# Retention's transpositions in one visit of three banks, HGRN2's heads side by side, and sample phases set apart: a decoder layer in fp32 on one core

## The chip, the core and the metric

The kernel runs on one core of a Trainium2 chip. The metric is the device time of one execution in microseconds (us). Five engines work side by side, each in its own instruction order: TensorE (PE, with its weight loads as PEld), VectorE (DVE), ScalarE (ACT), GpSimd (POOL) and SyncE (SP), which here only issues DMA transfers. They meet through semaphores. TensorE writes to PSUM, which has eight banks of 2 KB per partition.

## The reference

One layer of a hybrid decoder is computed in fp32 for two groups of requests: a prompt (16 learned meta tokens and 256 prompt tokens) and 8 sample tokens that continue states given as input.

```python
x = layer_norm(ALPHA * x + 0.5 * swiglu(x, f1_g, f1_u, f1_d), ln1_g, ln1_b)
m, s_ret, s_hg = token_mixer(x, pos, s_ret, s_hg, prompt, w_in, lb, hg_norm_g, w_out)
x = layer_norm(ALPHA * x + m, ln2_g, ln2_b)
x = layer_norm(ALPHA * x + 0.5 * swiglu(x, f2_g, f2_u, f2_d), ln3_g, ln3_b)

# token_mixer
q_r, k_r, v_r, g_r, q_h, f_h, i_h, g_h, a_r, a_h = jnp.split(x @ w_in, N_PROJ, axis=-1)
...
# retention (8 heads of 256) and HGRN2 (16 heads of 128), each over chunks:
S_new = jnp.exp(lg * C)[:, None, None] * S + jnp.einsum('bhjd,bhjv->bhdv', k_dec, v)
S_new = jnp.exp(b_last[:, :, 0, :, None]) * S + jnp.einsum('bhjd,bhjv->bhdv', k_dec, v)
...
o_r = head_layer_norm(...) * silu(g_r);  o_h = head_rms_norm(...) * silu(g_h)
y = sigmoid(a_r) * o_r + sigmoid(a_h) * o_h
return y @ w_out, s_ret, s_hg
```

D_MODEL is 2048, the FFN's inner width 5504. Outputs are y of prompt and samples, and the states of both mixers for prompt and samples. A sample's state is read from memory (retention 256x256 for each head and sample, HGRN2 128x128), updated by its token, read with its query, and written back.

## The kernel before

**Layout.** x lies transposed, features on the partitions and all tokens as 280 columns (16 meta, 256 prompt, 8 samples). Each fp32 value is split in two parts, so each 128x128 block of weights costs three matmuls: high weights by high x (L203), high by low (L204), low by high (L205). Weights are streamed in units of eight blocks: SP issues a load of 512 KB to `raw` (L176), ScalarE casts the high part `whi` (L177), VectorE subtracts for the low part `wlo` (L178). There are three buffers of each.

**Stages.** FFN 1 runs to about 740 us, then the input projection `w_in` with the mixers to about 1935 us, then `w_out` and FFN 2.

**The mixers run between the projection's matmuls.** There are eight units u, each of one retention head and two HGRN2 heads. For each unit `project` (L576) computes six groups of projections (f, q_h, i_h, q_r, k_r, v_r), then the gates of unit u−1. A group has two outputs, and 16 steps over the contracted dimension. After each step (six matmuls on 264 or 280 columns) it calls `pump` (L564): a pump counts down every running generator and lets those that are due emit their next piece. So `yield 11` in a mixer means: go on after 11 pumps. A steady unit has 160 pumps, 96 of its own groups and 64 of the gates of the unit before. Unit 0 has its groups of four outputs and no gates before it. What a mixer puts on TensorE between two projection matmuls is called a visit here.

`mix_hg` starts after the i group, `mix_ret` after the v_r group. `mix_hg` transposes v (`pt`), works through the levels of its chunked product (`pl`), transposes K for each head (`ptk`, L830), forms the prompt state (`pst`, L845), reads the samples' states (`pq`, L858), forms the output (`po`, L869 to L871) and its norm's sums (`pv`, L216). It does so for head 0, then for head 1: `ptk` of head 1 comes 31 pumps after that of head 0. In each round, after `ptk`, the head's eight sample states `smp` are updated: eight operations on ScalarE (L836) and eight on VectorE (L837), then the store. Head 1's states are loaded after `pq` of head 0 (L780 for the row of v, L781 for the state), into the same buffer. `mix_ret` transposes v and k for one half of the 256 features at a time, two banks each, in two visits four pumps apart (L894, L900); then scores (`psc`), prompt state (`psr`), outputs (`por`). Then come the samples in two halves of four: `load` (L915, L918), `update` (L923 on ScalarE, L926 on VectorE; two buffers `smr`, c = 0 and 1), `read` (`pqr`, L936). Then `pos`, the mean (`pm`) and the variance (`pvr`). All of that ends before the unit's gates have ended.

**What sets the order.** TensorE's order is the program's own. On ScalarE, VectorE, GpSimd and SP a scheduler places the instructions, and each engine then keeps to that order. PSUM is two pools of four banks: `acc` for the projections, `mx` in rotation for all banks of the mixers (`mx_bank`, L132), so that a fifth bank asked for is the first one again. `smr` has three buffers, which it shares with retention's decayed keys `ktr`; `smp` has one buffer for the state, which it shares with another tile of HGRN2.

## Time and profile before

| what | before |
|---|---|
| device time, median of 3 runs | 2792.39 us (2792.33 to 2794.63) |
| the profiled execution, own time | 2793.12 us |
| its span, first to last instruction | 2791.3 us |
| mean granted clock of TensorE | 0.998 |
| ACT, busy share | 49%, weight casts (L177) 909.5 us |
| DVE, busy share | 61%, weight subtractions (L178) 1063.6 us |
| HBM traffic | 191 GB/s over the span |

In the 40 slices of the span, VectorE is busy four to five tenths in the FFNs and six to seven in the mixers' stage, ScalarE four and five to six. Weights come at a steady 174 GB/s in the FFNs, and traffic rises to between 187 and 256 in the mixers' stage, where the samples' states go in and out besides.

In a row of the timeline stand start, duration, engine, line, operation, output<-input and shapes, and in brackets how long the engine had been idle before and what ended that. In a row of waits stand the waiting engine, tile and line, then what it waited for; then the total, the number of waits and the longest. Line numbers of the profile are those of the kernel before; in the changed kernel the lines of this stretch lie one or more further down.

### The profile page before, as it was taken

The page shows a single profiled execution, that of the slowest core. Times are in us where ns is not written, and L with a number is a line of the kernel's source. Part 1 is how long each engine was busy: PE and PEld are TensorE (multiplying, and loading weights), DVE is VectorE, ACT ScalarE, POOL GpSimd, SP SyncE. Part 2 cuts the span into 40 slices and gives each one's busy share as a digit, 9 for nine tenths or more (in the row PEclk, how much of TensorE's full clock was granted, in tenths as well). Part 3 has the DMA queues.
Part 4 walks back from the last instruction along what each step waited for, and adds up shares of the span by engine and source line. Part 5 has one row for each costly group of instructions (what it writes and reads, how often), then busy time and mean ns, then how long its engine had stood idle before and what let it go on. Part 6 is the DMA issues. An engine that isn't in the chain of part 4 may idle for free.

```text
span 2791.3 us, 55438 instructions
## 1 busy us (share of the span) xinstructions
PE 2761.4 (99%) x22992; PEld 2718.2 (97%) x22992; DVE 1711.4 (61%) x2957; ACT 1360.7 (49%) x2157; POOL 5.5 (0%) x47
## 2 busy tenths in 40 slices
PE   9999999999999899999999999999999999999999
PEld 9999999999999899899999998999999999999998
DVE  6444444555478677676767676766884444446554
ACT  5444434434355565656565656564554444444333
POOL 0000000000000000000000000000000000000000
PEclk9999999999999999999999999999999999999999
DMA  7555555555556576657675757575555565555664
GB/s 234 174 174 174 174 174 173 169 174 174 175 172 225 191 243 199 226 195 237 187 238 185 241 185 241 175 256 176 180 179 184 182 183 184 184 182 182 183 184 141
DMA packets 156460, 536.33 MB, mean 192 GB/s; under 512 B 18032, under 2 KB 27824, under 8 KB 156208
## 3 DMA queue, kind: packets, MB, share of 16 engines
q1 hardware_dynamic: 156064, 532.65, 60.3%
q8 instruction: 180, 2.95, 0.4%
q14 instruction: 72, 0.59, 0.1%
q10 hardware_dynamic: 144, 0.14, 0.0%
HBM read 502.12 MB, written 30.61 MB: 191 GB/s over the span
## 4 chain that ended last, share of the span: by engine, by line
PE 91%; DMA 3%; DVE 3%; ACT 2%; issue 1%; SPq 0%; ACTq 0%; DVEq 0%
PE up L204 12%; PE up L203 12%; PE up L205 12%; PE dn L204 6%; PE dn L203 6%; PE dn L205 6%; DMA smp<-in_sg 2%; PE pj_k_r L203 1%; DMA smr<-in_sr 1%; PE pj_v_r L203 1%; DVE wlo L178 1%; PE pj_f L204 1%; PE pj_f L205 1%; PE pj_k_r L204 1%; PE pj_k_r L205 1%; PE pj_v_r L204 1%
## 5 line engine op out<-in xcount | busy, mean ns | idle before, releaser
L178 DVE TENSOR_TENSOR wlo<-raw,whi 128x1024 fp32r<-128x1024 f32 (+1 forms) x871 | 1063.6, 1221 | 894.6 <-ACT whi L177 886.7
L177 ACT CAST whi<-raw 128x1024 fp32r<-128x1024 f32 (+1 forms) x871 | 909.5, 1044 | 1038.0 <-PE up L204 472.3
L204 PE MATMUL up<-x,whi 128*128 128x280 f32 (+1 forms) x2688 | 773.1, 288 | 0.0
L203 PE MATMUL up<-x,whi 128*128 128x280 f32 (+1 forms) x2688 | 766.3, 285 | 0.6 <-ACT whi L177 0.6
L205 PE MATMUL up<-x,wlo 128*128 128x280 f32 (+1 forms) x2688 | 764.0, 284 | 0.4 <-DVE wlo L178 0.4
L203 PEld LDWEIGHTS up<-x,whi 128*128 128x128 f32 x2688 | 504.9, 188 | 0.9 <-ACT whi L177 0.9
L205 PEld LDWEIGHTS up<-x,wlo 128*128 128x128 f32 x2688 | 505.0, 188 | 0.8 <-DVE wlo L178 0.7
L204 PEld LDWEIGHTS up<-x,whi 128*128 128x128 f32 x2688 | 504.5, 188 | 0.0
L204 PE MATMUL dn<-h,whi 128*128 128x280 f32 (+1 forms) x1376 | 395.6, 287 | 0.0
L203 PE MATMUL dn<-h,whi 128*128 128x280 f32 (+1 forms) x1376 | 392.6, 285 | 0.0
L205 PE MATMUL dn<-h,wlo 128*128 128x280 f32 (+1 forms) x1376 | 390.8, 284 | 0.0
L203 PEld LDWEIGHTS dn<-h,whi 128*128 128x128 f32 x1376 | 258.5, 188 | 0.1
L205 PEld LDWEIGHTS dn<-h,wlo 128*128 128x128 f32 x1376 | 258.5, 188 | 0.0
L204 PEld LDWEIGHTS dn<-h,whi 128*128 128x128 f32 x1376 | 258.3, 188 | 0.1
L203 PE MATMUL pj_g_h<-x,whi 128*128 128x264 f32 x256 | 76.6, 299 | 0.0
L203 PE MATMUL pj_g_r<-x,whi 128*128 128x264 f32 x256 | 76.2, 298 | 0.0
L203 PE MATMUL pj_k_r<-x,whi 128*128 128x280 f32 x256 | 75.1, 293 | 0.0
L205 PE MATMUL pj_i_h<-x,wlo 128*128 128x280 f32 x256 | 74.4, 291 | 0.5 <-DVE wlo L178 0.5
L204 PE MATMUL pj_i_h<-x,whi 128*128 128x280 f32 x256 | 74.5, 291 | 0.0
L204 PE MATMUL pj_k_r<-x,whi 128*128 128x280 f32 x256 | 74.5, 291 | 0.0
L204 PE MATMUL pj_v_r<-x,whi 128*128 128x280 f32 x256 | 74.5, 291 | 0.0
L203 PE MATMUL pj_v_r<-x,whi 128*128 128x280 f32 x256 | 74.5, 291 | 0.0
(377 smaller groups left out, 5207.0 us busy)
## 6 DMA issues: line engine op xcount, KB each, us to landing
raw<-in_w_up SPq DMA_DIRECT2D x341, 512.0 KB
raw<-in_w_in SPq DMA_DIRECT2D x320, 512.0 KB
raw<-in_w_dn SPq DMA_DIRECT2D x172, 512.0 KB
smr<-in_sr SPq DMA_DIRECT2D x32, 512.0 KB
out_srs<-smr SPq DMA_DIRECT2D x32, 512.0 KB
raw<-in_w_out SPq DMA_DIRECT2D x32, 512.0 KB
smp<-in_sg SPq DMA_DIRECT2D x16, 512.0 KB
vbr<-vrd SPq DMA_DIRECT2D x16, 512.0 KB
```

Of the source, the lines that this page charges most:

```text
L177: nc.scalar.copy(hi[:, j0:j1, :], raw[:, j0:j1, :])
L178: nc.vector.tensor_tensor(out=lo[:, j0:j1, :], in0=raw[:, j0:j1, :], in1=hi[:, j0:j1, :].bitcast(F32), op=ALU.subtract)
L203: nc.tensor.matmul(o, wh, h, start=k == 0, stop=False)
L204: nc.tensor.matmul(o, wh, l, start=False, stop=False)
L205: nc.tensor.matmul(o, wl, h, start=False, stop=k == nk - 1)
```

## The change

Four things are done together. The arithmetic stays the same, and TensorE keeps its number of instructions.

1. Retention's 12 transpositions of a unit go into one visit: v's blocks into bank `pv`, k's into `pk`, both tails into a third, `pt`. Each bank is emptied 256 or 512 columns at a time, in place of 128 or 256.
2. In `mix_hg` the two heads go side by side: `ptk` of both, then `pst` of both, `po` of both, `pv` of both. Only the samples stay one after the other. `update` becomes a function: head 0's stands ahead of `ptk`, head 1's 12 pumps after its load. Some tiles get a copy for the second head.
3. Retention's sample phases are set apart from the outputs by APART pumps: 34 in units 2 to 6, 32 in unit 0, 52 in unit 1, none in unit 7. They then run in the next unit's f, q_h and i_h groups.
4. HGRN2's start in unit 1 waits 24 pumps in place of 36.

```diff
+APART = {0: 32, 1: 52, 7: 0, 2: 34}
...
-            start(mix_hg(c0 // 2, st["f"], st["k"], st["q"], v), {0: 3, 2: 36}.get(c0, 3))
+            start(mix_hg(c0 // 2, st["f"], st["k"], st["q"], v), {0: 3, 2: 24}.get(c0, 3))
...
+        def update(h, vb, sm):
+            for b in range(NS):
+                nc.scalar.activation(sm[:, b, :], sm[:, b, :], AF.Copy, scale=fs[:, h, b : b + 1])
+                nc.vector.scalar_tensor_tensor(
+                    out=sm[:, b, :], in0=vb[:, b, :], scalar=ks[:, h, b : b + 1], in1=sm[:, b, :],
+                    op0=ALU.mult, op1=ALU.add)
+            nc.sync.dma_start(O["sgs"][2 * u + h], sm)
...
         Tt = dT[P]
+        update(0, *samples)
         yield W_LEVEL
         on = tmp("on_h", (P, 2, TL), bufs=2)
         on_h[u] = on
+        kt = [tmp("kth", (P, 2, P)) for h in range(2)]
         for h in range(2):
-            kt = tmp("kth", (P, 2, P))
             pt = mx_bank("ptk")
             for b, (t0, n) in enumerate(((NMETA, P), (NMETA + P, P), (0, NMETA))):
                 nc.tensor.transpose(pt[:n, b * P : (b + 1) * P], K[:, h, t0 : t0 + n], ident)
-            nc.scalar.copy(kt, pt[:, : 2 * P].rearrange("p (b f) -> p b f", b=2))
-            stack(lambda r: km3[r, :], pt[:NMETA, 2 * P : 3 * P], 64)
-
-            vb, sm = samples
-            for b in range(NS):
-                nc.scalar.activation(sm[:, b, :], sm[:, b, :], AF.Copy, scale=fs[:, h, b : b + 1])
-                nc.vector.scalar_tensor_tensor(
-                    out=sm[:, b, :], in0=vb[:, b, :], scalar=ks[:, h, b : b + 1], in1=sm[:, b, :],
-                    op0=ALU.mult, op1=ALU.add)
-            nc.sync.dma_start(O["sgs"][2 * u + h], sm)
-            yield 11
-
-            S = tmp("Sh", (P, 3, P))
+            stack(lambda r: km3[r, h, :], pt[:NMETA, 2 * P : 3 * P], 64)
+            nc.scalar.copy(kt[h], pt[:, : 2 * P].rearrange("p (b f) -> p b f", b=2))
+        yield 11
+
+        S = [tmp("Sh", (P, 3, P)), tmp("Sh1", (P, 3, P), tag="K")]
+        for h in range(2):
             pst = mx_bank("pst")
-            nc.tensor.matmul(pst[:, 0:P], km3, vm3[:, h, :], start=True, stop=True)
-            nc.tensor.matmul(pst[:, P : 2 * P], kt[:, 0, :], vt[:, h, 0, :], start=True, stop=True)
-            nc.tensor.matmul(pst[:, 2 * P : 3 * P], kt[:, 1, :], vt[:, h, 1, :], start=True, stop=True)
-            nc.scalar.copy(S[:, 0, :], pst[:, :P])
+            nc.tensor.matmul(pst[:, 0:P], km3[:, h, :], vm3[:, h, :], start=True, stop=True)
+            nc.tensor.matmul(pst[:, P : 2 * P], kt[h][:, 0, :], vt[:, h, 0, :], start=True, stop=True)
+            nc.tensor.matmul(pst[:, 2 * P : 3 * P], kt[h][:, 1, :], vt[:, h, 1, :], start=True, stop=True)
+            nc.scalar.copy(S[h][:, 0, :], pst[:, :P])
             for b in range(2):
                 nc.vector.scalar_tensor_tensor(
-                    out=S[:, b + 1, :], in0=S[:, b, :], scalar=Tt[:, h, b : b + 1],
+                    out=S[h][:, b + 1, :], in0=S[h][:, b, :], scalar=Tt[:, h, b : b + 1],
                     in1=pst[:, (b + 1) * P : (b + 2) * P], op0=ALU.mult, op1=ALU.add)
-            nc.sync.dma_start(O["sgp"][2 * u + h], S[:, 2, :])
-            yield 10
+            nc.sync.dma_start(O["sgp"][2 * u + h], S[h][:, 2, :])
+        yield 4
+        os = tmp("osh", (P, 2, P))
+        for h in range(2):
             pq = mx_bank("pq")
             for b in range(NS):
                 j = 32 * (b % 4)
                 nc.tensor.matmul(
-                    pq[j : j + 32, :P], qdh[:, h, 32 * b : 32 * b + 32], sm[:, b, :],
+                    pq[j : j + 32, :P], qdh[:, h, 32 * b : 32 * b + 32], samples[1][:, b, :],
                     start=b < 4, stop=b >= 4, tile_position=(0, j))
-            os = tmp("osh", (P, P))
-            nc.scalar.copy(os, pq[:, :P])
+            nc.scalar.copy(os[:, h, :], pq[:, :P])
             if h == 0:
                 samples = load(1)
-            yield 3
+                yield 12
+                update(1, *samples)
+                yield 11
+        yield 4
+        hilo = []
+        for h in range(2):
             po = mx_bank("po")
             for b in range(2):
                 o = po[:, b * P : (b + 1) * P]
                 nc.tensor.matmul(o, vt[:, h, b, :], acc[:, (2 * h + b) * P : (2 * h + b + 1) * P], start=True, stop=False)
-                nc.tensor.matmul(o, S[:, b, :], Q[:, h, b * P : (b + 1) * P], start=False, stop=True)
-            nc.tensor.matmul(po[:, SEQ:TL], os, sel, start=True, stop=True)
+                nc.tensor.matmul(o, S[h][:, b, :], Q[:, h, b * P : (b + 1) * P], start=False, stop=True)
+            nc.tensor.matmul(po[:, SEQ:TL], os[:, h, :], sel, start=True, stop=True)
             sq = tmp("sqh", (P, TL))
             nc.scalar.activation(sq, po[:, :TL], AF.Square)
-            hilo = tmp("hhi", (P, TL), dt=F32R), tmp("hlo", (P, TL), dt=F32R)
-            split(*hilo, sq)
+            hilo.append((tmp("hhi", (P, TL), dt=F32R), tmp("hlo", (P, TL), dt=F32R)))
+            split(*hilo[h], sq)
             nc.scalar.copy(on[:, h, :], po[:, :TL])
-            yield 7
-            pv = mx_bank("pv")
-            sums(pv[:, :TL], hilo)
-            r = rsqrt(lambda name: tmp(name, (P, TL)), pv[:, :TL], 1.0 / P, eps_h)
+        yield 7
+        pv = [mx_bank("pv") for h in range(2)]
+        for h in range(2):
+            sums(pv[h][:, :TL], hilo[h])
+        for h in range(2):
+            r = rsqrt(lambda name: tmp(name, (P, TL)), pv[h][:, :TL], 1.0 / P, eps_h)
             mul(on[:, h, :], on[:, h, :], r)
         done_h.add(u)
...
-        for c in range(2):
-            pt = mx_bank("pt")
+        pv, pk, pt = mx_bank("pt"), mx_bank("pt"), mx_bank("pt")
+        for x, p, p2 in ((v, pv, pt[:, : 2 * P]), (k, pk, pt[:, 2 * P :])):
             for b, (t0, n) in enumerate(BLOCKS):
-                nc.tensor.transpose(pt[:n, b * P : (b + 1) * P], v[:, c, t0 : t0 + n], ident)
-            split(vh[:, :, c, :], vl[:, :, c, :], pt[:, : 2 * P].rearrange("p (b f) -> p b f", b=2))
-            nc.scalar.copy(vtl[: BLOCKS[2][1], c, :], pt[: BLOCKS[2][1], 2 * P : 3 * P])
-            stack(lambda r: vs3[r, c, :], vtl[:NB2, c, :], 32)
-            pt = mx_bank("pt")
-            for b, (t0, n) in enumerate(BLOCKS):
-                nc.tensor.transpose(pt[:n, b * P : (b + 1) * P], k[:, c, t0 : t0 + n], ident)
-            for b in range(2):
-                kb, d = pt[:, b * P : (b + 1) * P], dec[:, b, u : u + 1]
-                nc.vector.tensor_scalar(out=kh[:, b, c, :], in0=kb, scalar1=d, scalar2=None, op0=ALU.mult)
-                nc.vector.scalar_tensor_tensor(
-                    out=kl[:, b, c, :], in0=kb, scalar=d, in1=kh[:, b, c, :].bitcast(F32), op0=ALU.mult, op1=ALU.subtract)
-            ktl = tmp("ktl", (P, P))
-            nc.scalar.activation(ktl[:NB2, :], pt[:NB2, 2 * P : 3 * P], AF.Copy, scale=dec[:NB2, 2, u : u + 1])
-            stack(lambda r: ks3[r, c, :], ktl[:NB2, :], 64)
-            yield 4
+                for c in range(2):
+                    at = (2 * b + c if b < 2 else c) * P
+                    nc.tensor.transpose((p if b < 2 else p2)[:n, at : at + P], x[:, c, t0 : t0 + n], ident)
+        flat = [x.rearrange("p b c f -> p (b c f)") for x in (vh, vl)]
+        split(*flat, pv)
+        nc.scalar.copy(vtl[: BLOCKS[2][1]], pt[: BLOCKS[2][1], : 2 * P].rearrange("p (c f) -> p c f", c=2))
+        stack(lambda r: vs3[r], vtl[:NB2], 32)
+        for b in range(2):
+            kb, d = pk[:, 2 * b * P : 2 * (b + 1) * P], dec[:, b, u : u + 1]
+            hi, lo = (x[:, b].rearrange("p c f -> p (c f)") for x in (kh, kl))
+            nc.vector.tensor_scalar(out=hi, in0=kb, scalar1=d, scalar2=None, op0=ALU.mult)
+            nc.vector.scalar_tensor_tensor(out=lo, in0=kb, scalar=d, in1=hi.bitcast(F32), op0=ALU.mult, op1=ALU.subtract)
+        ktl = tmp("ktl", (P, 2, P))
+        nc.scalar.activation(
+            ktl[:NB2], pt[:NB2, 2 * P :].rearrange("p (c f) -> p c f", c=2), AF.Copy, scale=dec[:NB2, 2, u : u + 1])
+        stack(lambda r: ks3[r], ktl[:NB2], 64)
+        yield 8
...
-        first = load(0)
+        apart = APART.get(u, APART[2])
+        if not apart:
+            first = load(0)
         psc = mx_bank("psc")
...
+        if apart:
+            yield apart
+            first = load(0)
+            yield 10
         update(0, *first)
         yield 6
         os = tmp("osr", (P, 256))
```

The first place is on ScalarE in unit 3, around the visit with `ptk` and retention's transpositions; `whi` are weight casts, `v` retention's values, `kth` and `km3` copies of `ptk`, `vtr`, `vtl` and `ktl` copies of retention's banks. Before:

```order
L624 COPY v_16392<-pj_v_r8_16249 128x280
L177 CAST whi170_16538<-raw170_16537 128x1024
L625 COPY v_16392<-pj_v_r9_16250 128x280
L831 COPY kth_16422<-ptk_16423 128x256
L559 CAST km3_8603<-ptk_16423 16x128
L560 CAST km3_8603<-ptk_16423 16x128
L210 CAST vtr_16448<-pt_16455 128x2x128
L177 CAST whi171_16596<-raw171_16595 128x1024
```

After:

```order
L178 CAST whi170_16469<-raw170_16468 128x1024
L626 COPY v_16347<-pj_v_r9_16188 128x280
L560 CAST km3_8603<-ptk_16379 16x128
L561 CAST km3_8603<-ptk_16379 16x128
L560 CAST km3_8603<-ptk_16387 16x128
L561 CAST km3_8603<-ptk_16387 16x128
L843 COPY kth_16377<-ptk_16379 128x256
L211 CAST vtr_16395<-pt_16402 128x512
L843 COPY kth_16378<-ptk_16387 128x256
L911 COPY vtl_16397<-pt_16404 24x256
L919 ACTIVATE ktl_16427<-pt_16404,dec_87 16x256
L178 CAST whi171_16521<-raw171_16520 128x1024
```

Both heads' `km3` and `kth` now come together, the casts for `km3` ahead of the copy `kth`, and `vtr` stands between the two copies.

The same place on TensorE, after the change (before, `ptk` of head 0 was followed by two banks of three transpositions, and two more came four pumps later):

```order
L841 MATMUL ptk_16379<-ident_77,K_15812 128x128 x2
L841 MATMUL ptk_16379<-ident_77,K_15812 16x128
L841 MATMUL ptk_16387<-ident_77,K_15812 128x128 x2
L841 MATMUL ptk_16387<-ident_77,K_15812 16x128
L908 MATMUL pt_16402<-ident_77,v_16347 128x128 x4
L908 MATMUL pt_16404<-ident_77,v_16347 24x128 x2
L908 MATMUL pt_16403<-ident_77,k_r_16178 128x128 x4
L908 MATMUL pt_16404<-ident_77,k_r_16178 24x128 x2
```

Five banks are written in one visit; the third of retention's, `pt_16404`, is the fifth.

The second place is the second halves of the samples in unit 3. First ScalarE, around the update of retention's second half, c = 1 (`smr`). Before:

```order
L836 ACTIVATE smp_16769<-smp_16769,fks_15877 128x128 x2
L177 CAST whi180_17077<-raw180_17076 128x1024
L836 ACTIVATE smp_16769<-smp_16769,fks_15877 128x128 x3
L923 ACTIVATE smr_16829<-smr_16829 128x1024
L177 CAST whi181_17117<-raw181_17116 128x1024
L848 COPY Sh_17028<-pst_17029 128x128
```

After, for the same samples:

```order
L178 CAST whi188_17275<-raw188_17274 128x1024
L1005 COPY osr_17188<-pqr_17189 128x256
L178 CAST whi189_17317<-raw189_17316 128x1024
L936 ACTIVATE smr_17202<-smr_17202 128x1024
L597 ACTIVATE f_17265<-pj_f10_17114 128x280
L178 CAST whi190_17347<-raw190_17346 128x1024
L597 ACTIVATE f_17265<-pj_f11_17115 128x280
```

The update of `smr` stood behind five of head 1's `smp`; it now stands among the next unit's weight casts and f, and no `smp` is near.

Then SP, where head 1's states (`smp`) and retention's second half (`smr`) are loaded. Before:

```order
L915 DMA vbr_16826<-vrd_16562 128x1024
L780 DMA smp_16769<-vh1d_15912 128x1024
L176 DMA raw179_17016<-in_w_in 128x1024
L781 DMA smp_16769<-in_sg 128x1024
L918 DMA smr_16829<-in_sr 128x1024
L176 DMA raw180_17076<-in_w_in 128x1024
```

After:

```order
L177 DMA raw177_16815<-in_w_in 128x1024
L782 DMA smp_16630<-vh1d_15850 128x1024
L783 DMA smp_16630<-in_sg 128x1024
L177 DMA raw178_16845<-in_w_in 128x1024
L928 DMA vbr_17199<-vrd_16493 128x1024
L177 DMA raw179_16885<-in_w_in 128x1024
L931 DMA smr_17201<-in_sr 128x1024
```

Between the two transfers of `smp` there was a weight load, now there is none, and the weight load follows.

The third place is ScalarE at the end of the next unit's i_h group, after the change, where `pvr` is retention's variance and `v` now HGRN2's value. Before, `rv` and `rr` of `pvr` stood in the gates, ahead of the next unit's f, and nothing but weight casts stood around `v`.

```order
L178 CAST whi197_17669<-raw197_17668 128x1024
L233 ACTIVATE rv_17566<-pvr_17563,eps_h_81 128x264
L611 COPY v_17582<-pj_i_h10_17431 128x280
L178 CAST whi198_17699<-raw198_17698 128x1024
L234 ACT_TABLE_LOAD
L234 ACTIVATE rr_17567<-rv_17566 128x264
L612 COPY v_17582<-pj_i_h11_17432 128x280
L723 COPY vth_17626<-pt_17628 128x256
```

The reciprocal root for retention, with its table load, has moved to between the two halves of `v`.

More of the change, by code (lines that the diff above doesn't have):

```diff
@@ L551, in trunk @@
             ss3 = tmp("ss3", (P, NMETA), dt=F32R)
-            vm3, km3 = tmp("vm3", (P, 2, P), dt=F32R), tmp("km3", (P, P), dt=F32R)
-            for t in (vs3[:, 0, :], vs3[:, 1, :], ks3[:, 0, :], ks3[:, 1, :], vm3[:, 0, :], vm3[:, 1, :], km3, ss3):
+            vm3, km3 = tmp("vm3", (P, 2, P), dt=F32R), tmp("km3", (P, 2, P), dt=F32R)
+            for t in (vs3[:, 0, :], vs3[:, 1, :], ks3[:, 0, :], ks3[:, 1, :], vm3[:, 0, :], vm3[:, 1, :], km3[:, 0, :], km3[:, 1, :], ss3):
                 nc.scalar.copy(t, qdh[:, 0, : t.shape[-1]])
@@ L712, in queries @@
                     mul(right(s), right(s), t2[:, :, m - mq :, 0].unsqueeze(3).to_broadcast([P, 2, mq, s]))
-                vt = tmp("vth", (P, 2, 3, P))
+                vt = tmp("vth", (P, 2, 2, P))
+                vs = tmp("vsh", (P, 2, P))
                 vrow = []
@@ L721, in mix_hg @@
                     nc.scalar.copy(vt[:, h, 0:2, :], pt[:, : 2 * P].rearrange("p (b f) -> p b f", b=2))
-                    nc.scalar.copy(vt[:NMETA, h, 2, :], pt[:NMETA, 3 * P :])
+                    nc.scalar.copy(vs[:NMETA, h, :], pt[:NMETA, 3 * P :])
                     stack(lambda r: vm3[r, h, :], pt[:NMETA, 2 * P : 3 * P], 32)
-                    vrow.append(rows_out(vt[8:16, h, 2, :], P, f"vh{h}"))
+                    vrow.append(rows_out(vs[8:16, h, :], P, f"vh{h}"))
                 yield 1
```

2 rows, old and new, of the table rows are left out of this document.

## The prediction

> **What bounds the kernel now.** The page comes first, for which engine fills the span.
>
> ```profile
> span 2791.3 us, 55438 instructions
> PE 2761.4 (99%) x22992; PEld 2718.2 (97%) x22992; DVE 1711.4 (61%) x2957; ACT 1360.7 (49%) x2157; POOL 5.5 (0%) x47
> ```
>
> TensorE is busy 99% of the span, and the change leaves its matmuls and transpositions the same in number and almost the same in size. So what it can win is TensorE's waiting, and what it can lose is new waiting. Busy time hides part of this: matmuls overlap, and a matmul recorded as running may itself be waiting for its weights. So the second view is the waits of TensorE's weight loads (columns: total us, times, longest us).
>
> ```profile
> PEld pqr L936 <- DVE smr L926: 19.8, 25, 1.4
> PEld pm L216 <- ACT rhi L210: 7.1, 1, 7.1
> PEld po L871 <- ACT osh L862: 2.6, 3, 1.9
> PEld pst L845 <- issue: 1.9, 4, 0.5
> PEld pj_g_r L205 <- DVE wlo L178: 1.8, 3, 1.3
> ```
>
> The reader is to see one large item, pqr, the read of the updated retention states, and one long single wait, pm. That these rows give the whole price is seen in the third view, the timeline around one such read in the fourth unit (start, duration, engine).
>
> ```profile
> 1299.00 1.05 ACT L923 ACTIVATE smr<-smr 128x1024 f32<-128x1024 f32 x1
> 1299.59 1.40 DVE L837 SCALAR_TENSOR_TENSOR smp<-smp,fks 128x128 f32<-128x128 f32 x5
> 1299.80 0.28 PE L205 MATMUL pj_a_r<-x,wlo 128*128 128x264 f32 x1
> 1300.01 0.64 PE L936 MATMUL pqr<-smr,qdr 128*32 128x256 f32 x8
> 1300.90 0.48 DVE L926 SCALAR_TENSOR_TENSOR smr<-vbr,k_r,smr 128x256 f32<-128x256 f32 x1
> 1301.30 1.22 DVE L178 TENSOR_TENSOR wlo<-raw,whi 128x1024 fp32r<-128x1024 f32 x1
> 1301.43 0.62 PE L936 MATMUL pqr<-smr,qdr 128*32 128x256 f32 x2 [0.79 <-DVE smr L926]
> 1302.43 1.27 DVE L926 SCALAR_TENSOR_TENSOR smr<-vbr,k_r,smr 128x256 f32<-128x256 f32 x3
> 1302.97 1.41 PE L936 MATMUL pqr<-smr,qdr 128*32 128x256 f32 x6 [0.91 <-DVE smr L926]
> 1304.31 0.39 PE L203 MATMUL pj_g_r<-x,whi 128*128 128x264 f32 x1
> ...
> 1284.07 0.28 PE L205 MATMUL pj_a_h<-x,wlo 128*128 128x264 f32 x1
> 1284.28 1.07 PE L936 MATMUL pqr<-smr,qdr 128*32 128x256 f32 x16
> 1285.29 0.39 PE L203 MATMUL pj_g_h<-x,whi 128*128 128x264 f32 x1
> ```
>
> From the last projection matmul to the next one this second read takes 1304.31 − 1299.80 = 4.51 us; the unit's first read, whose states are ready, takes 1285.29 − 1284.07 = 1.22. The stall is 3.29 us, though the gaps printed add up to 1.70 only. Six units at this much would be 19.7; the weight-load row has 19.8. The reason is in front of it: VectorE updates HGRN2's second head (L837) before the retention state (L926), and that head's update began late.
>
> ```profile
> 1290.02 0.40 ACT L836 ACTIVATE smp<-smp,fks 128x128 f32<-128x128 f32 x1 [4.15 <-DMA smp<-in_sg]
> ...
> 1280.01 0.33 SPq L780 DMA_DIRECT2D smp<-vh1d  x1
> 1284.21 0.33 SPq L176 DMA_DIRECT2D raw<-in_w_in  x1
> 1284.60 0.42 SPq L781 DMA_DIRECT2D smp<-in_sg  x1
> ```
>
> ScalarE stood 4.15 us waiting for a state whose load was issued behind a weight load that waited for its buffer.
>
> The pm wait of the first unit has the same root (ScalarE held 7.28 us), and it costs more than itself:
>
> ```profile
> 921.52 0.70 ACT L836 ACTIVATE smp<-smp,fks 128x128 f32<-128x128 f32 x2 [7.28 <-DMA smp<-in_sg]
> ```
> ```profile
> 929.30:939.40 10.10, 6.28 (x27) 6.10 (x28) 6.63 (x17) 4.14 (x10) 0.00 (x0) 0.50 0.52 157
> 940.00:950.00 10.00, 10.00 (x91) 9.65 (x91) 7.68 (x18) 4.78 (x8) 0.00 (x0) 1.00 0.48 141
> 1299.80:1304.30 4.50, 2.80 (x19) 0.77 (x17) 4.16 (x11) 2.62 (x4) 0.00 (x0) 1.00 0.91 310
> ```
>
> These are rows of stretches (length, TensorE's busy time and matmuls, …, then the granted clock). After the 7.1 us wait the clock is 0.50 for 10.1 us; 27 matmuls take 6.28 us busy, against 27 × 10.00/91 = 2.97 at full clock: 3.3 us more. Over a read that stalls 3.3 us the clock stays 1.00.
>
> **The change, part by part.** The sum is made against the profiled execution's own 2793.12 us (span 2791.3 and 1.8 around it); it lies 0.7 above the median of the runs, 2792.39, which I take off at the end.
>
> *Parted sample phases: the gain.* Retention's reads move by some 45 pumps (0.73 us each) into the next unit's f, q and i groups, where no HGRN2 sample update runs. For units 0 to 6 the stall goes. What is late next there: the second half's load is issued after read 0, 18 pumps (13 us) ahead of read 1; the last load took 1290.02 − 1284.60 = 5.42 us to its use, and its update 1.05 on ScalarE and four operations on VectorE; I see some 4 us of slack. In the last unit the reads stay where they were, and I keep half of its stall, 1.5. **Gain: 19.8 − 1.5 = 18.3.**
>
> *The first unit.* pm now comes later than its inputs by a whole group: **7.1**, and the half clock that followed: **3.3**.
>
> *Small waits.* pst waited for km, which was queued behind the update that now stands ahead of the transpositions: **1.9** goes. po (2.6) and pj_g_r (1.8) waited for copies in crowded stretches; I take half, **2.2**, between nothing and 4.4. Gains: 32.8.
>
> *Five banks in a pool of four.* In units 2 to 7 HGRN2's six transpositions (two banks) and retention's twelve (three banks) share one visit. The fifth bank is the first one again, and can be written only when it is copied out.
>
> ```profile
> 1256.82 0.49 PE L830 MATMUL ptk<-ident,K 128*128 128x128 f32 x3
> 1257.14 0.49 PE L894 MATMUL pt<-ident,v 128*128 128x128 f32 x3
> ...
> 1260.57 0.28 PE L205 MATMUL pj_a_r<-x,wlo 128*128 128x264 f32 x1
> 1260.69 0.49 PE L894 MATMUL pt<-ident,v 128*128 128x128 f32 x3
> 1261.27 0.37 PE L203 MATMUL pj_g_r<-x,whi 128*128 128x264 f32 x1
> ```
> ```profile
> 1257.34 0.37 ACT L831 COPY kth<-ptk 128x256 f32<-128x256 f32 x1 [1.25 <-PE ptk L830]
> 1257.61 0.25 ACT L559 CAST km<-ptk 16x128 fp32r<-16x128 f32 x1
> 1257.88 0.26 ACT L560 CAST km<-ptk 16x128 fp32r<-16x128 f32 x1
> ```
>
> Three transpositions take 0.32 us, so TensorE wants the fifth bank after ten: 1.08 us from the first. ScalarE starts 0.52 after the first (1257.34 − 1256.82), and by the new order does four km casts (0.27 each) before the copy kth (0.37): 0.52 + 1.08 + 0.37 = 1.97. Stall 0.9, with the signal's way 0.95; six units: **cost 5.7**. Bounds: nothing (the bank is free in time) and 2.0 each (a weight cast of 1.05 in front).
>
> *HGRN2's v earlier against retention's end.* Retention's last statistics now end in the last pump of the next unit's i group, so on ScalarE rv, a table load and rr stand around the copies of v that the transpositions need three pumps later.
>
> ```profile
> 1292.76 0.37 ACT L831 COPY kth<-ptk 128x256 f32<-128x256 f32 x1
> 1293.15 1.28 ACT L233 ACT_TABLE_LOAD   x1
> 1294.45 0.43 ACT L233 ACTIVATE rr<-rv 128x264 f32<-128x264 f32 x1
> 1294.78 1.03 ACT L177 CAST whi<-raw 128x1024 fp32r<-128x1024 f32 x1
> ```
>
> By starts: v's first half 0.27 (as kth goes by), weight cast 0.94, table load 1.30, rr 0.33, v's second half 0.37; from some 0.3 after the group's end that is ready at 3.5. TensorE wants it after 18 matmuls (18 × 0.125 = 2.25) and four transpositions (0.44): 2.7. Stall 0.85 in units 3 to 7: **cost 4.25**, between nothing (rv's row early enough to pull all ahead) and 2.0 each.
>
> A page weighs in here: the Trainium skill, "ScalarE: Activation LUTs", section "What ACT_TABLE_LOAD costs", gives a switch 1283 ns and about 1380 ns of drain besides. By that, as an estimate, the stall would be 2.2 and the sum 7 us higher. The trace agrees on the 1.28 but shows no drain: kth ends at 1293.13, the load starts at 1293.15, and rr 0.02 us after its end. I stay with the trace.
>
> *Merged visits.* The visit of six transpositions above took 1261.27 − 1260.57 = 0.70, of which 0.12 is the projection's own pitch: 0.58 for 6 × 0.109 = 0.65. Each visit gives some 0.08 back by overlap, so fewer visits lose it: a steady unit has 22 now and 18 after. 4 × 7 × 0.08 = **cost 2.3**. TensorE thus gains nothing by merging itself. Emptying banks 512 columns at a time saves ScalarE and VectorE a few fixed costs (32 instructions fewer), nothing on the path while they are at 49% and 61%.
>
> *The ends.* In unit 1 and the last unit the new order crowds VectorE and ScalarE around pvr and the sample states: I estimate 2 and 1 us, unit 0 0.7, from waits of 0.5 to 1.9 in the rows above; bounds nothing and twice as much. **Cost 3.7.**
>
> *The updates' new place.* Head 0's update stands before the transpositions: it issues eight operations on ScalarE and eight on VectorE and one store on SP; behind it on ScalarE wait v's copies and the weight casts. Its state was loaded eleven pumps before, at the same place as now: nothing. Head 1's load is issued with no weight load between the two transfers, so some 4.2 us earlier (1284.60 − 1280.01 less one issue); its seven operations on ScalarE stand ahead of a weight cast that TensorE needs. By the groups between, that cast is late if the state lands more than some 10 us after pq of head 0; 5.42 after issue makes it about 6. I cost it at nothing; without the cover see the third rival.
>
> Costs 5.7 + 4.25 + 2.3 + 3.7 = 16.0; gains 32.8; net 16.8. 2793.1 − 16.8 − 0.7 = 2775.6. **Forecast 2776.**
>
> **The rivals.**
>
> *Banks and v dearer.* If a weight cast stands in front at both places (2.0 each instead of 0.95 and 0.85): 6 × 1.05 + 5 × 1.15 = 12 more, 2788; half of it, the middle of this case, 2782. For it: ScalarE has a 1.05 us cast in nearly every 3 us. Against: the order puts the casts behind the copies.
>
> *Nothing new waits.* Without the costs for the bank, v and the ends: 2776 − 13.6 = 2762. For it: ScalarE idles half the time. Against: both stalls come from fixed orders.
>
> *The second head's state lands late: slower.* If a load that is not covered takes ScalarE as much longer as in the first unit (7.28 − 4.15 = 3.1 more than 5.42) and is issued no earlier than now, it lands 13.3 us after pq, 3.3 past the point of 10, with the weight cast behind it; in seven units 23 us: 2776 + 23 = 2799. It decides from 13.2 us after pq on. For it: the same wait has held ScalarE in the rows above. Against: the weight load between the two transfers is gone in the new order, and so is the competing retention load.
>
> *It doesn't do what it says.* The reads move, but the updates are placed by the scheduler; if the second half's update is again issued last moment, the 3.3 us return in the next unit: 2776 + 18.3 = 2794, no change. For it: the first half's update stays where it was. Against: that one is ready early, and the second has 13 us.
>
> *The clock.* If each of the eleven new waits of about 0.9 us halved the clock as the 7.1 us wait did, each would cost 5 us (half of 10.1): 2776 + 55 = 2831. The rows speak against it: 1.00 over a read with two waits of 0.8 and 0.9. The Trainium skill, "TensorE: Matmul & The Clock Gate", section "A second HAM failure mode: psum-queue depth-cycling", warns of just this: banks cycled with frequent small idles make the clock swing. By this trace that happens only after the long wait.
>
> **How the numbers follow.** Forecast 0.46 (2768 to 2781), dearer 0.16, nothing new 0.14, not what it says 0.13, late state 0.08, clock 0.03. A measurement of this kernel tells about 0.2% from no change, 2786.8 to 2798.0. Faster: the first three but for 0.02, and 0.03 of the fourth: 0.77. Slower: 0.07 of the late state, 0.03 clock: 0.10. Same: 0.13. The range reaches from nothing new, 2761, to 2790; it leaves out most of the fourth, the late state and the clock, and a little below.
>
> **What would show it.** In the changed profile: pqr gone from TensorE's waits except in the last unit, and pm's; the clock 1.00 at 930 to 940; a wait of about 1 us in the retention transpositions' visit for the copy kth, and in HGRN2's v transpositions for the second copy of v; smp on ScalarE with no DMA wait over some 2 us ahead of a weight cast. The prediction is wrong if weight casts or their subtractions release TensorE's projections in many places, or if pqr still waits for smr by more than 1 us per unit.

## The result, and the profile after

The changed kernel takes 2766.52 us (median of 5 runs, 2765.46 to 2769.23); the kernel before, in the runs beside it, 2794.63 (2792.33 to 2801.90). The ratio is 0.9896, 95% interval 0.9882 to 0.9910. The forecast was 2776 in a range of 2761 to 2790: the direction and the range hold, and the gain is larger than forecast: 26.6 us between the two profiled executions (2793.12 and 2766.52), in place of 16.8.

The page of the changed kernel, then the rows of its weight loads' waits that answer to those of before (us in total, times, longest):

```profile
span 2764.7 us, 55247 instructions
PE 2748.8 (99%) x22992; PEld 2713.3 (98%) x22992; DVE 1702.2 (62%) x2901; ACT 1358.2 (49%) x2102; POOL 5.4 (0%) x47
```
```profile
PEld pt L908 <- ACT kth L843: 5.1, 6, 0.9
PEld pt L722 <- ACT v L612: 3.7, 5, 0.7
...
PEld pvr L217 <- DVE rlo L212: 2.0, 2, 1.1
PEld pvr L217 <- ACT rhi L211: 1.9, 1, 1.9
```

Matmuls are the same in number. The waits of pqr, pm, po, pst and pj_g_r are all gone; in their place stand two small new ones that recur in the steady units, the bank (kth, units 2 to 7) and HGRN2's v (units 3 to 7), and one larger in unit 1 (pvr). A second read now looks like a first one, in the timeline of the changed kernel (1323.03 − 1321.82 = 1.21 us):

```profile
1321.82 0.28 PE L206 MATMUL pj_q_h<-x,wlo 128*128 128x264 f32 x1
1322.03 1.07 PE L949 MATMUL pqr<-smr,qdr 128*32 128x256 f32 x16
1323.03 0.39 PE L204 MATMUL pj_q_h<-x,whi 128*128 128x264 f32 x1
```

The wait for the bank, in unit 3:

```profile
1244.07 0.28 PE L206 MATMUL pj_a_r<-x,wlo 128*128 128x264 f32 x1
1244.19 0.82 PE L841 MATMUL ptk<-ident,K 128*128 128x128 f32 x6
1244.84 0.82 PE L908 MATMUL pt<-ident,v 128*128 128x128 f32 x6
1245.81 0.37 ACT L843 COPY kth<-ptk 128x256 f32<-128x256 f32 x1
1246.23 0.88 PE L908 MATMUL pt<-ident,k_r 128*128 128x128 f32 x6 [0.57 <-ACT kth L843]
1246.86 0.37 PE L204 MATMUL pj_g_r<-x,whi 128*128 128x264 f32 x1
1247.07 0.28 PE L205 MATMUL pj_g_r<-x,whi 128*128 128x264 f32 x1
1247.19 0.28 PE L206 MATMUL pj_g_r<-x,wlo 128*128 128x264 f32 x1
```

The visit takes 2.79 us; 18 transpositions at 0.109 need 2.0. The stall is 0.79 us. It comes after twelve transpositions, ahead of k: the wait falls on k's bank. The order had been read to put it on that of the tails, for which the program asks last. And at v, in unit 4:

```profile
1341.82 1.28 ACT L234 ACT_TABLE_LOAD   x1
1342.69 0.28 PE L206 MATMUL pj_q_r<-x,wlo 128*128 128x264 f32 x1
1343.44 0.37 ACT L612 COPY v<-pj_i_h 128x280 f32<-128x280 f32 x1
1343.87 0.66 PE L722 MATMUL pt<-ident,v 128*128 128x128 f32 x4 [0.45 <-ACT v L612]
1344.28 0.37 PE L204 MATMUL pj_q_r<-x,whi 128*128 128x264 f32 x1
```

This visit takes 1.59 us, the same eight transpositions without the wait 0.92: a stall of 0.67.

### The profile page after: what moved, and what is told of

Read it like the earlier page. It is cut to its first block, busy times and chain, and to the rows that moved or that the text cites. A ratio compares the mean times of both kernels' runs of the same rounds, so it can differ in the third digit from the quotient of the medians.

```text
span 2764.7 us, 55247 instructions
## 1 busy us (share of the span) xinstructions
PE 2748.8 (99%) x22992; PEld 2713.3 (98%) x22992; DVE 1702.2 (62%) x2901; ACT 1358.2 (49%) x2102; POOL 5.4 (0%) x47
## 4 chain that ended last, share of the span: by engine, by line
PE 98%; ACT 2%; DVE 0%; issue 0%; DMA 0%; ACTq 0%; DVEq 0%
PE up L205 12%; PE up L204 12%; PE up L206 12%; PE dn L205 6%; PE dn L204 6%; PE dn L206 6%; PE pj_k_r L204 1%; PE pj_v_r L204 1%; PE pj_i_h L204 1%; PE pj_i_h L205 1%; PE pj_f L204 1%; PE pj_k_r L205 1%; PE pj_k_r L206 1%; PE pj_v_r L205 1%; PE pj_v_r L206 1%; PE pj_g_r L204 1%
## 5 line engine op out<-in xcount | busy, mean ns | idle before, releaser
L206 PE MATMUL pj_k_r<-x,wlo 128*128 128x280 f32 x256 | 74.4, 290 | 0.0
```

The source lines that it names most:

```text
L206: nc.tensor.matmul(o, wl, h, start=False, stop=k == nk - 1)
```

## The experiments

Each is timed beside the kernel before on one chip, but not all on the same chip (the kernel before took 2791.0 to 2794.6 us in the groups), so between rows the ratios compare better than the times.

| kernel | median us | ratio to before, 95% interval |
|---|---|---|
| the change | 2766.5 | 0.9896 (0.9882 to 0.9910) |
| parting alone | 2773.1 | 0.9934 (0.9918 to 0.9951) |
| the change without parting | 2764.5 | 0.9903 (0.9888 to 0.9918) |
| heads alone | 2760.7 | 0.9882 (0.9868 to 0.9897) |
| heads alone, pvr later | 2753.9 | 0.9866 (0.9849 to 0.9882) |
| without parting, load late | 2772.0 | 0.9924 (0.9909 to 0.9938) |
| before, load early | 2785.0 | 0.9963 (0.9951 to 0.9976) |
| before, update first | 2794.3 | 1.0003 (0.9989 to 1.0017) |
| the change, old transpositions | 2758.4 | 0.9880 (0.9866 to 0.9895) |
| the change, retention 2 pumps later | 2758.6 | 0.9880 (0.9866 to 0.9895) |
| old transpositions, APART 36 | 2754.6, again 2754.7 | 0.9863 (0.9846 to 0.9879), 0.9869 (0.9854 to 0.9884) |
| the same, visits split | 2760.1 | 0.9881 (0.9866 to 0.9895) |

**Which part brings the gain.** Parting alone, put into the kernel before:

```diff
+APART = {0: 32, 1: 52, 7: 0, 2: 34}
...
-                first = load(0)
+                apart = APART.get(u, APART[2])
+                if not apart:
+                    first = load(0)
...
+                if apart:
+                    yield apart
+                    first = load(0)
+                    yield 10
                 update(0, *first)
```

> The kernel before with only the sample phases of retention set apart by APART pumps; heads, transpositions and start waits as before. If the parting is what removes the wait of the second reads (my prediction), pqr leaves TensorE's waits: the visits of pqr are all near 1.21 us, 20.7 us less in sum, and head 1's late update no longer matters to retention: about 2768 to 2774 us beside 2793 to 2795. If instead it is HGRN2's new order (head 1's state loaded with no weight load in between, updated earlier) that removes it, the reads here are still late by 3 us in their new place and the time stays near 2790. In both cases the small waits of pst and po (1.9 and 2.6 us in the weight-load rows) should stay, as ScalarE still waits some 4 us for smp.

The pqr waits go wherever the reads are parted. The last unit isn't, and there it stays, while the changed kernel's last unit, which is not parted either, shows none. The two reads, first with parting alone (1847.96 − 1843.45 = 4.51 us), then in the changed kernel (1846.41 − 1845.20 = 1.21):

```profile
1843.45 0.28 PE L206 MATMUL pj_a_r<-x,wlo 128*128 128x264 f32 x1
...
1845.09 0.62 PE L937 MATMUL pqr<-smr,qdr 128*32 128x256 f32 x2 [0.79 <-DVE smr L927]
1846.62 1.41 PE L937 MATMUL pqr<-smr,qdr 128*32 128x256 f32 x6 [0.91 <-DVE smr L927]
1847.96 0.39 PE L204 MATMUL pj_g_r<-x,whi 128*128 128x264 f32 x1
```
```profile
1845.20 0.28 PE L206 MATMUL pj_a_r<-x,wlo 128*128 128x264 f32 x1
1845.41 1.07 PE L949 MATMUL pqr<-smr,qdr 128*32 128x256 f32 x16
1846.41 0.39 PE L204 MATMUL pj_g_r<-x,whi 128*128 128x264 f32 x1
```

So the heads' new order must do the same by itself. The change without parting:

```diff
-APART = {0: 32, 1: 52, 7: 0, 2: 34}
+APART = {2: 0}
```

> The changed kernel with APART 0 in all units, so retention's sample phases come right after its outputs as before. Parting is needed: the second reads wait some 3.3 us again in units 2 to 6 (16 to 20 us in sum), time 2782 to 2788. Heads alone suffice (for this speaks that in the changed kernel the last unit is not parted and its second read takes 1.21 us): pqr does not wait, and since retention's end (pvr) then no longer falls on HGRN2's v, the 3.4 us of waits at v go too: 2760 to 2766.

No row of pqr waiting for smr is left (one second read of six takes 1.40 us, the others 1.21), and 2764.5 us, no slower than with parting. The next kernel has the old transpositions too, so that only the heads' order (and unit 1's start) is left of the change:

```diff
-APART = {0: 32, 1: 52, 7: 0, 2: 34}
+APART = {2: 0}
...
-                pv, pk, pt = mx_bank("pt"), mx_bank("pt"), mx_bank("pt")
...
+                for c in range(2):
+                    pt = mx_bank("pt")
```

> The kernel before with only HGRN2's heads side by side (and the start wait of unit 1): retention's transpositions as before, APART 0. If the heads' order alone brings the gain: 2764.5 of the unparted kernel less the bank wait, 4.7 to 5: about 2760, and the parting is worth the difference to the old transpositions with parting (2758.4), some 1 us. If the parting is needed besides, 2775 or more.

2760.7: the heads alone bring no less than the whole change. What it still waits for is mainly pvr (0.79 us in most of six units), which one number mends:

```diff
-                yield 9
+                yield 12
                 pv = mx_bank("pvr")
```

> The heads-only kernel (old transpositions, no parting) with retention's variance 12 pumps behind the mean in place of 9, as its visit of pvr took 1.16 us in place of 0.37 in six units, waiting for rlo. If the heads' order is enough by itself, this comes to 2760.7 less 4.7, 2756, as good as the kernel with heads, parting and APART 36 (2754.6), and the parting adds nothing but pumps of slack. If the parting has a worth of its own beyond the waits that the trace shows, this stays 3 us or more above 2754.6.

2753.9 (2753.6 to 2758.9): as good as the best kernel with parting, beside which it ran. The parting is enough by itself for the reads, but with the heads side by side it adds nothing that these times show. The slack is thin without it: in the traced execution, the slowest of the four, three second reads still take 2.09, 1.89 and 1.34 us (units 2, 6 and 7) in place of 1.21.

**What made the reads late.** The prediction blamed head 1's late load. Three kernels move the load or the update alone. First, without parting, pq of head 0 and the load behind it 6 pumps later:

```diff
-                yield 4
+                yield 10
...
-                        yield 12
+                        yield 6
                         update(1, *samples)
```

> The unparted kernel (APART 0) with pq of head 0, and so the load of head 1's states, 6 pumps (4.4 us) later, at pump 120 where it was before the change; heads still side by side, update(1) still called at pump 126. If it is the time of this load that decides whether head 1's update stands in the way of retention's second half, pqr waits again, 2 to 3.3 us in units 2 to 7: 2776 to 2784. If the order of the heads does it in another way, pqr does not wait: 2762 to 2767.

The second reads still take 1.21 us in all steady units, although the state came nearly as late: in unit 3 head 1's update starts on ScalarE 10.9 us ahead of the second read (1283.91 and 1294.79), in the kernel before 9.8 (1290.02 and 1299.80). Beside the change without parting, five steady units together grow by 1.0 us. Of the 7.5 us in all, most is in unit 1, where the row of pm's wait has 5.1 (one wait; 1.1 before the move) and the clock is 0.50 for 6.8 us behind it. Then the mirror image in the kernel before, head 0's pq and the load 6 pumps earlier, the rest as it was:

```diff
-                    yield 10
+                    yield 4 if h == 0 else 10
...
-                    yield 3
+                    yield 9 if h == 0 else 3
```

> The kernel before with one thing moved: pq of HGRN2's head 0, and with it the load of head 1's states, 6 pumps (4.4 us) earlier, at pump 114 as in the changed kernel; heads one after the other, transpositions and sample phases as before. If the late load (and the time that ScalarE stands in front of it) is what makes the second reads late, pqr leaves the waits in units 2 to 7: 19 us less, 2770 to 2775, with no other part of the change. If the side-by-side order is needed, pqr still waits and the time is 2785 or more.

Between the two: 9 us faster, not 19. The load counts, but the second reads still take 2.2 to 2.4 us in units 2 to 7, although in unit 3 head 1's last update on ScalarE ends at 1283.64, some 15 us ahead of the read (1298.91). And other waits come beside pqr's, in the weight loads' rows of this kernel:

```profile
PEld pj_g_r L205 <- DVE wlo L178: 8.5, 10, 1.3
PEld pqr L936 <- DVE smr L926: 5.1, 16, 1.6
PEld pst L845 <- issue: 4.6, 6, 2.0
```

The move is not the load alone: retention's own load comes later by it (the first update of the second half starts on ScalarE at 1289.23, after a wait of 3.53 us for its state; before at 1280.93).

Last, in the kernel before, only the update's place in the program:

```diff
+                    if h == 0:
+                        update(0, *samples)
...
                     yield 7
+                    if h == 0:
+                        update(1, *samples)
                     pv = mx_bank("pv")
```

> The kernel before with the update of HGRN2's head 1 called ahead of pv of head 0 and ptk of head 1 in place of behind them; TensorE's order and all loads as before (its states are loaded as late as before). By the order, five of the eight smp operations leave the places right ahead of retention's smr on ScalarE and VectorE. If it is only the order of the updates that makes the second reads late, pqr's 3.3 us go: about 2773. If it is a backlog of ScalarE, which has waited 4 us for the late state and then has the same work ahead of smr in whatever order, smr starts at the same time and only VectorE's 1.4 us of smp leave the way: a stall of about 2 us stays, 2785 to 2788.

Not faster at all (1.0003). pqr falls from 19.8 to 3.2 us in the weight loads' rows, but pst, which had 1.9, now waits in front of it, in unit 3 for 3.15 us:

```profile
1299.96 0.28 PE L205 MATMUL pj_a_r<-x,wlo 128*128 128x264 f32 x1
1303.39 0.30 PE L849 MATMUL pst<-vm,km 128*128 128x128 f32 x1 [3.15 <-DVE km L561]
```
```profile
PEld pst L849 <- issue: 15.8, 6, 3.3
```

The wait has changed its name and nearly kept its size. Behind three of the six pst waits the clock also falls to 0.50, for 3.4 to 6.8 us, and the second reads take 1.7 to 2.2 us. This fits a backlog: work that is late on ScalarE and VectorE, whatever its order. The stretches show how full they are (length, busy TensorE, weight loads, VectorE, ScalarE, GpSimd, then the clock), first of the kernel before over the 14 us that end with the second read, then of the heads-only kernel up to its second read:

```profile
1290.00:1304.00 14.00, 12.12 (x98) 10.20 (x95) 12.47 (x27) 12.34 (x24) 0.00 (x0) 1.00 0.74 233
```
```profile
1271.30:1285.30 14.00, 14.00 (x134) 13.43 (x136) 10.68 (x20) 9.33 (x18) 0.00 (x0) 1.00 0.83 298
```

Before, ScalarE and VectorE are busy 88 and 89% there, though over the span only 49 and 61%: head 1's and retention's updates, head 0's norm with its table load, head 1's ptk and the weight casts all fall due together, after ScalarE has stood 4 us. Whatever is last in line makes TensorE wait. Side by side, the heads' ptk and norms lie outside it.

The busy share alone does not decide it. The same stretch with the heads side by side and the load late, where nothing waits, and of the kernel before with the load early, where the read loses 1.2 us:

```profile
1282.00:1296.00 14.00, 14.00 (x136) 12.94 (x136) 12.01 (x25) 10.01 (x23) 0.00 (x0) 1.00 0.93 306
```
```profile
1287.30:1301.30 14.00, 12.20 (x94) 9.99 (x92) 10.88 (x22) 10.95 (x17) 0.00 (x0) 1.00 0.80 260
```

VectorE is busy 86% in the first and 78% in the second. What differs is what stands on ScalarE between head 1's first update and that of retention's second half. In the kernel before it takes 8.98 us (1290.02 to 1299.00), with head 0's norm and its table load, head 1's ptk copies and three weight casts in between. Side by side, with the late load, it takes 3.58:

```profile
1283.91 2.16 ACT L788 ACTIVATE smp<-smp,fks 128x128 f32<-128x128 f32 x7 [0.93 <-DMA smp<-in_sg]
...
1287.49 1.05 ACT L936 ACTIVATE smr<-smr 128x1024 f32<-128x1024 f32 x1
```

With the early load the norm, the ptk copies and the casts still stand directly in front of that update (1290.19 to 1295.87). This is read from the traces; no run moves the norm or the ptk copies alone.

**What the new order costs.** The old transpositions in the changed kernel (two visits, two banks each):

```diff
-                pv, pk, pt = mx_bank("pt"), mx_bank("pt"), mx_bank("pt")
...
+                for c in range(2):
+                    pt = mx_bank("pt")
...
+                    yield 4
```

> The changed kernel with retention's transpositions as before: one half of the features at a time, two banks each, two visits four pumps apart. ptk of both heads and the first half then make four banks. If the wait for the copy kth is for the fifth bank, it goes: 0.79 us x 6 = 4.7 us less, about 2762. If fewer visits lose overlap (0.08 each, as I predicted), another 0.6 less; if a visit more costs nothing, none. If the wider emptying saves TensorE something, the time is not below 2766.

8.1 us below the change by the medians, 8.7 by the spans of the two traced executions (2764.7 and 2756.0): more than 4.7. The rest is in units 0 and 1 in the trace, behind retention's one long visit: the pvr visit of unit 1 falls from 3.53 to 0.36 us. Whether the length of that visit or its 512-column copies crowded what followed, no run tells. The other way out is to keep the three banks and start retention two pumps later:

```diff
-                    start(mix_ret(c0 // 2, st["q_r"], st["k_r"], v), 3)
+                    start(mix_ret(c0 // 2, st["q_r"], st["k_r"], v), 5)
```

> The changed kernel with retention's start 5 pumps after its v group in place of 3, so that its transpositions come 1.5 us after HGRN2's ptk, in a visit of their own; all of retention moves by two pumps. Bank wait: kth (ready 0.8 us after TensorE wanted the bank) is done by then, 4.7 us less; pvr falls two pumps later, one into the next group, so that its rv no longer stands ahead of the copies of v: the v wait (0.67 us x 5) may go or not. 2759 to 2763. If the wait is for something else than the bank, it stays: 2766.

2758.6: the bank wait is gone and so is the one at v, since the reciprocal root behind pvr now stands on ScalarE after both copies of v. The same move of pvr with the old transpositions:

```diff
-APART = {0: 32, 1: 52, 7: 0, 2: 34}
+APART = {0: 32, 1: 52, 7: 0, 2: 36}
```

> The changed kernel with retention's old transpositions and APART 36 in place of 34 in units 2 to 6, so that pvr falls into pump 49, after the i group, and the reciprocal root no longer stands between the copies of v. Both new waits are then gone: 2758.4 (old transpositions alone) less 0.67 us x 5 = 3.4, so about 2755. If the wait at v has another cause than the place of the root and its table load, it stays and the time is 2758.

2754.6 as expected; of TensorE's waits, two rows are left:

```profile
PE pw L461 <- DVE eps_h L154: 1.1, 1, 1.1
PE pvr L217 <- DVE rlo L212: 0.7, 1, 0.7
```

The price of a visit: the same kernel with pst, po and pv in visits of their own; po and pv likewise:

```diff
                     nc.sync.dma_start(O["sgp"][2 * u + h], S[h][:, 2, :])
-                yield 4
+                    yield 1
+                yield 3
```

> The same kernel as the one beside it with APART 36, but pst, po and pv of the two heads in visits of their own, one pump apart: 24 visits more, the same matmuls. If fewer visits lose overlap, as I predicted (0.08 us each), these win 2.0 us. If the first projection matmul after a visit gives the 0.08 back (its follower starts 0.20 us later instead of 0.12), nothing changes but what new waits show: within 0.5 us, and the sum of a visit and the interval after it is the number of its matmuls times their pitch either way.

No gain of 2 us: 5.5 us slower. The overlap that a visit has at its start is given back behind it: in the rows of the bank wait above, the projection's second matmul starts 1247.07 − 1246.86 = 0.21 after the first, the third 0.12 after that. The loss is new waits, mainly these of the weight loads, and a half clock of 3.4 us behind pm's:

```profile
PEld pj_g_r L206 <- DVE wlo L179: 2.8, 4, 1.0
...
PEld pm L217 <- DVE rlo L212: 1.4, 1, 1.4
```

And the best kernel once more, beside the heads-only one:

> The same kernel as the one with old transpositions and APART 36, beside the heads-only kernel on one chip: 2754.6 again within 2.

2754.7 (2753.8 to 2755.7). Both it and the heads-only kernel with pvr later beat the change, by 12 us in the medians and by 8 to 9 in the gain over the kernel before beside each (28.1, 36.3 and 37.1).

## Why the prediction was right, and where it was not

| term of the sum | predicted | measured |
|---|---|---|
| pqr | −18.3 | −19.8, the whole row (−20.7 by the lengths of the visits) |
| pm and the half clock behind it | −10.4 | −10.4, both gone |
| small waits of po, pst, pj_g_r | −4.1 | −6.3, all three rows gone |
| bank | +5.7 | +4.7 (6 × 0.79) |
| v | +4.25 | +3.4 (5 × 0.67) |
| ends: units 0, 1, 7 | +3.7 | +6.0 |
| merged visits | +2.3 | 0 |
| net | −16.8 | −22.4 of 26.6 |

- **The pqr gain** was right in size but for the last unit, of whose stall half was kept because its reads stay in place; it went whole. (The "Six units at this much" were five stalls of 3.30, one of 2.89 in unit 7 and one of 1.30 in unit 1.) "For units 0 to 6 the stall goes" was put down to the parting, and the parting does suffice (19 us alone), but it was not needed: the heads' order alone takes the stall away too, which the sum put at nothing. That the size held is partly luck, since both were in the change. The step that failed is the wait's cause, the late load of head 1: left late with the heads side by side it costs the reads nothing, and early without them it brings 9 us where the parting alone brings 19.
- **The first unit** came out as forecast: no pm wait there, and the clock is 1.00 from 924 to 960.
- **Small waits**: half of po's and pj_g_r's was kept as a guess; all went. po's were no part of the crowded stretch: ahead of it, in units 3, 4 and 6, osh stood on ScalarE behind a weight cast and an update of retention's states (smr) that had waited 4.00, 4.47 and 5.78 us for its load. Parting alone and the heads alone both take them away; those of pst stay with parting alone (2.4 us in its rows).
- **Bank and v** were right in mechanism and place. The bank is wanted after twelve transpositions, not ten, so its wait is 0.79, not 0.95. At v the load of the table lasts 1.28 and rr follows it 0.01 us later, so no drain shows here either, which the prediction weighed after the Trainium skill ("ScalarE: Activation LUTs", "What ACT_TABLE_LOAD costs").
- **The ends**: unit 1 was mis-sized. Its pvr visit waits 3.2 us and the clock behind it is 0.50 for 3.4 us, some 1.4 of which are lost, against 2 in the sum; the last unit's pvr 0.9, unit 0's visit of twelve 0.4.
- **Merged visits**: this term failed too. "Each visit gives some 0.08 back by overlap" looked at the visit alone and not at the matmul interval behind it, which takes it again (0.21 in place of 0.12). Nor are the wider copies 32 instructions fewer: the pages have 55 fewer on ScalarE and 56 on VectorE, off TensorE's path as the prediction said.
- Of the 26.6 us, 4.2 are not in the table's rows; 1.2 of them are single waits of pj_i_h and pj_q_r for wlo before (0.7 and 0.5). Most of the rest is in the rows' own sizes: from the last projection matmul to the next, the visits of before lose more than the rows say, pqr 20.7 in place of 19.8, pm 7.7 in place of 7.1, po 3.1 in place of 2.6, pst 2.2 in place of 1.9. Some 0.7 stays open.
- Of **the rivals**, the late state did not come. ScalarE still waits for smp, 21.6 us in all (47.0 before) and up to 4.1 with a weight cast soon behind, more than the 2 us that the prediction allowed for, but no projection waits for whi or wlo in the changed kernel's rows. The clock stayed whole over all eleven small waits, in a stretch of the changed kernel from unit 2 to 7:

```profile
1100.00:1850.00 750.00, 744.32 (x6582) 721.32 (x6581) 533.77 (x1087) 440.14 (x813) 1.62 (x11) 1.00 0.68 221
```

The Trainium skill, "TensorE: Matmul & The Clock Gate", section "A second HAM failure mode: psum-queue depth-cycling", describes a clock that swings when TensorE idles briefly but often between groups of matmuls. In this trace it does not swing with stalls of 0.7 and 0.8 us, two in a unit of 139 us.

## What to carry to other kernels

When several engines wait for one another in a short stretch, the row of waits names only what is last in line: before pricing its removal, look at the stretch, not at the span, and list what the other engines' fixed orders hold between the late input and the waiting read; a busy share alone does not tell (here VectorE at 86% without a wait, at 78% with one). Here, moving a large piece out of the stretch took the wait away, and moving an update within it renamed the wait. Merging TensorE's side work into fewer visits saves nothing by itself here, and a visit that needs one bank more than the pool has waited for a copy, 0.79 us each time.

## What the runs showed of the hardware

In the trace before, the clock fell only after the wait of 7.1 us. The runs show it after shorter waits, and not at a fixed length. In the kernel before, the reads that stalled 3.3 us with matmuls in between ran on at 1.00, and so did a wait of po of 1.7 us. In the kernel with the update first, pst's 3.15 us without a matmul were followed, in unit 2, by

```profile
1158.60:1162.50 3.90, 3.90 (x26) 2.40 (x26) 2.12 (x4) 1.55 (x2) 0.00 (x0) 0.50 0.85 230
```

so the wait that moved from pqr to pst became dearer. In unit 1 of the change two waits of 1.73 and 0.90 us with one matmul between them were enough, and in the kernel with split visits two of 0.42 and 1.25 (for each the waits, and then the stretch behind them, with the clock third from the end):

```profile
973.78 0.39 PE L217 MATMUL pvr<-rhi,ones_r 128*128 128x264 f32 x1 [1.73 <-ACT rhi L211]
975.07 0.39 PE L217 MATMUL pvr<-rlo,ones_r 128*128 128x264 f32 x1 [0.90 <-DVE rlo L212]
```
```profile
975.10:978.60 3.50, 3.50 (x36) 3.08 (x37) 3.44 (x11) 2.84 (x6) 0.00 (x0) 0.64 0.88 240
```
```profile
1848.96 0.39 PE L217 MATMUL pm<-rhi,ones_r 128*128 128x264 f32 x1 [0.42 <-ACT rhi L211]
1850.60 0.41 PE L217 MATMUL pm<-rlo,ones_r 128*128 128x264 f32 x1 [1.25 <-DVE rlo L212]
```
```profile
1850.80:1854.20 3.40, 3.40 (x17) 3.40 (x17) 2.42 (x7) 1.86 (x4) 0.00 (x0) 0.51 0.56 154
```

The Trainium skill, "TensorE: Matmul & The Clock Gate", section "Why this matters for your kernels", asks for no idle gaps over about 3 us between bursts of matmuls. The 3.15 us agree. The two pairs of shorter waits lie below that and cost clock as well; what decides between them and the 1.7 us that cost nothing stays open.
